# More on-chip tiles in a two-layer encoder: B's outputs kept in SBUF, spare tiles for four kinds of intermediate, a descriptor scratch of 1 KB

## The chip, the cores and the metric

The kernel runs on one core of one Trainium2 chip. The metric is the time of one execution on the device in microseconds. The core's engines are named as in the profile: PE (TensorE, with PEld for its weight loads), DVE (VectorE), ACT (ScalarE), POOL (GpSimd) and SP (SyncE, which here only issues transfers). SBUF is the on-chip memory of 128 partitions, PSUM the eight banks in which TensorE accumulates.

## The reference

A trunk of two layers over 1024 tokens of width 1024, in float32. Each layer has four groups of attention heads side by side, whose outputs (256 columns each) are joined, and an MLP of width 4096:

```python
h = rms_norm(x, norm1_g[l]); proj = h @ w_in[l]
y_a = mla_mixer(...)    # A: 4 heads, dense, keys and values from a latent of 128
y_b = diff_mixer(...)   # B: 4 heads, dense, difference of two softmaxes, rms_norm per head
y_c = swa_mixer(...)    # C: 4 query heads on 2 key heads, window of +-128 tokens, sink logits
y_d = na_mixer(...)     # D: 4 heads, 8 x 16 neighbourhood on a grid 64 wide, position bias
mix = concatenate([rms_norm(y_a), y_b, rms_norm(y_c), rms_norm(y_d)])
x = x + mix @ w_out[l]
h = rms_norm(x, norm2_g[l])
x = x + square(relu(h @ w_up[l])) @ w_down[l]
```

After the last layer there is one more rms_norm.

## The kernel before

Everything is held transposed: features on the 128 partitions, tokens along the row. A float32 product is made in three passes of a reduced format: each operand is split into a high part (a copy on ACT, L193) and a low part (a subtraction on DVE or POOL, L187), and `passes` (L219 to L221) issues high x high, high x low and low x high into one PSUM bank.

**Order of a layer.** The projections of B come first. Then four attention groups follow, B, D, C, A, and each is woven with other matrix work as filler: B with the projections for A's latent and for D, D with the projections for C and the expansion of A's latent (`latp`, `kan`, `qan`), C and A with those parts of the output projection whose inputs are there (`groups_bd`, which adds onto four tiles `sum`). Projections go through a tile `part`, are split into a tile `both` (high and low side by side) and are stored from there to DRAM as `qd`, `kd`, `vd`, `qc`, `kan`, `qar` and so on; the heads load them back as `stack` and `v`. Then come the rest of the output projection, the MLP's first half and its second half.

**A banded head (D and C).** Per block kb of 128 keys: the scores four blocks ahead (L987, bank `sb`, three banks), a softmax on DVE and ACT into `p`, up to three transposes of `p` on PE (L996, bank `tr`, two banks), the split of the result into `pth` (ACT) and `ptl` (DVE), and the product with the values (L1008 and L1009) into the one bank `pv`. After block 4 the bank is full: `pv_out` copies its upper half to a tile `pvt` (ACT, L757), DVE adds both halves into the output tile `y` (in C `yc`, from another pool), PE zeroes the bank again (L1037), and the blocks 3 and 4, which were held, are applied to the second half. `pvt` shares its tiles with `ptl`.

**B's outputs.** When a pair of B's heads is finished, `sub_norm` normalises its tile `y`, stores it to DRAM as `yb` (SP, L166) and lets the tile go; `mix_b` loads it back into a tile `rz` (L159) during D and splits it, scaled, into `mixh` and `mixl` (ACT L196, DVE L197) for the output projection. B has two such tiles, D two, A two; the pool holds two tiles `y` in all.

**The MLP's first half.** The product with `w_up` is made by a scheme of seven products for two by two blocks. For each of 16 column groups q seven block products (p1 to p7, "12", "11" and so on) are accumulated in banks and moved to result tiles `ev` of 128 x 512 (ACT L1237 for the second product, L1247 and L1256 for two others), which are activated (DVE L1220, ACT L1222), combined by four subtractions (L187, `ev<-ev`) and stored to DRAM as `acts`, by ACT's queue or SP's (L1226). The groups 0 and 1 run together, product by product; from group 2 on they run one by one, with the last three products of the group before in between.

**What sets the order.** In the attention a scheduler orders each engine's instructions by a modelled timeline and by the priorities that the weave gives. In the MLP the order on PE is the order in which the code is written; the other engines are scheduled. A tile is taken from a pool of `bufs` tiles of its tag; the first write into a tile waits until the work on its former content is done, loads and stores included.

Of the kernel before, what the change touches and what calls it, by code (L numbers as in the profile page):

```python
# [13 lines left out]
F = mybir.dt.float32  # L14
R = mybir.dt.float32r
# [4 lines left out]
P = 128  # L20
S = 1024
# [123 lines left out]
class Trunk:  # L145
# [436 lines left out]

    def both(self):

        return self.pp.tile([P, 2, 512], R, tag="both", bufs=2, name="both")

    def emit_parts(self, src, dst, rows=slice(0, P), scale=None):

# [114 lines left out]
    def latent_up(self, l, lat, rows, qa, ka, va):  # L703
# [30 lines left out]

        w0 = self.weights(d["w_lat"][l, 0])
        yield from two([w0[0], both(w0[1])], parts[0:2], self.ev_rope(tabs, qr))
        plain = lambda r, dst: self.ev_plain(r, self.to_parts(dst))
        yield from two([w0[2], both(w0[3])], parts[0:2], plain(rq, qn[:, 0]))
        w1 = self.weights(d["w_lat"][l, 1])
        yield from two(w1[2:3], parts[2:3], plain(rkv, kn[:, 0]))  # L740
        w2 = self.weights(d["w_lat"][l, 2])
        for t in range(2):
            yield from two(w2[t:t + 1], parts[2:3], self.ev_plain(rkv, self.to_values(va[2 * t:2 * t + 2])))
        yield from two([w1[0], both(w1[1])], parts[0:2], plain(rq, qn[:, 1]))
        yield from two(w1[3:4], parts[2:3], plain(rkv, kn[:, 1]))

# [6 lines left out]

    def pv_out(self, pv, y, j, half, grid=False):

        t = self.ap.tile([P, 512], R, tag="ptl", bufs=3, name="pvt").bitcast(F)[0:64]
        self.nc.scalar.activation(t, pv[64:128], AF.Copy)  # L757
        a, b, o = pv[0:64], t, y[j * 64:(j + 1) * 64]
        if grid:
            a, b = (v.rearrange("p (b r c) -> p b r c", b=4, r=16) for v in (a, b))  # L760
            o = o.rearrange("p (r b c) -> p b r c", b=8, c=8)[:, 4 * half:4 * half + 4]
        else:
            o = o[:, half * 512:half * 512 + 512]
        self.tt(o, a, b, ALU.add)
# [25 lines left out]
        return self.ap.tile([P, S], F, tag="rz", bufs=2, name="rz")  # L790

    def ypair(self):
        return self.ap.tile([P, S], F, tag="y", bufs=2, name="y")

    def ptile(self):
        return self.ap.tile([P, S], F, tag="p", bufs=self.NP, name="p")
# [5 lines left out]

    def transposed(self, w):

        return [self.ap.tile([P, 512], R, tag=n, bufs=3, name=n)[:, :w] for n in ("pth", "ptl")]


    def softmax(self, passes, qt, z, scale):
# [106 lines left out]
    def sub_norm(self, y, rz, out):  # L915

        nc = self.nc
        self.tt(y, y, rz, eng=nc.gpsimd)
        yield
        sq = self.rz_tile()  # L920
        nc.scalar.activation(sq, y, AF.Square)
        r = self.rstd_cols(sq, 64, self.pairs, eng=nc.gpsimd)
        yield
        r = self.rows_of(r)
        yield
        rb = self.rz_tile()
        for h2 in range(2):
            self.spread(rb[h2 * 64:(h2 + 1) * 64], r, h2, 2)
        yield
        self.tt(y, y, rb, eng=nc.gpsimd)  # L930
        kept = self.dram.tile([P, S], F, tag="yb", bufs=2, name="yb")
        self.keep(kept, y)
        out.append(kept)
        yield

    def attn_a(self, l, qa, kn, krd, va, ys):
# [177 lines left out]

    def mix_b(self, mix, ys, g):
        for t, y in enumerate(ys):
            yt = self.rz_tile()
            self.load(yt, y)
            yield
            mix[t] = self.mixed(yt, g)  # L1120
            yield

    def mix_group(self, mix, k0, ys, g, eng=None):
# [34 lines left out]
    def piece(self, tag, dt=F, name=None):  # L1158


        pool = self.late if tag in ("c", "ev") else self.early
        return pool.tile([P, 512], dt, tag=tag, bufs={"raw": 10, "ev": 9}.get(tag, 8), name=name or tag)

    def rows_split(self, t, src, scale=None):

# [335 lines left out]
```

## Time and profile before

| | before |
|---|---|
| time, median of 3 runs | 2698.26 us (2697.42 to 2702.37) |
| the profiled execution's time | 2701.14 us |
| its span, first to last instruction | 2698.9 us |
| mean granted clock of TensorE | 0.969 |
| TensorE busy | 2545.4 us, 94% |
| VectorE, ScalarE, GpSimd busy | 1944.6, 1438.1, 1151.6 us |
| moved by DMA | 389.18 MB |

A row of the timeline gives start, duration, engine, line, operation, output <- inputs, size, and in brackets the idle time just before it and what ended it. A row of the waits gives who waited for what: total, times, longest, in us. A row of the table by stage gives the stage's bounds and length, each engine's busy time with its count of instructions, the granted clock as a share of full speed, the mean busy share of the DMA engines, and GB/s. In layer 0, D and C run from about 330 to 505 us and the MLP from 700; in layer 1, D and C from about 1660 to 1835 and the MLP from 2030.

### The profile page before, as it was taken

The numbers are of one execution on the slowest core, as the hardware profiler recorded it, in microseconds if no ns is written. First come the engines' busy times: TensorE is split into PE (matmuls) and PEld (weight loads), VectorE is DVE, ScalarE is ACT, GpSimd is POOL, SyncE is SP. The second block draws the span as 40 slices with busy tenths as digits, with TensorE's granted clock in tenths as the row PEclk, the third lists the DMA queues.
The fourth block names the chain that finished last, engine by engine and source line by source line (L and its number), as shares of the span: only waits on it lengthen the run. The fifth ranks groups of instructions, "written<-read, shape, count | busy, mean of one in ns | idle before, by whom it ended". The sixth has DMA issues, their size and how long they took to land.

```text
span 2698.9 us, 37585 instructions
## 1 busy us (share of the span) xinstructions
PE 2545.4 (94%) x12296; PEld 2109.5 (78%) x12296; DVE 1944.6 (72%) x3368; ACT 1438.1 (53%) x2591; POOL 1151.6 (43%) x816
## 2 busy tenths in 40 slices
PE   8999988999889999999999999789998999999997
PEld 6778876787778887888877788677886788778886
DVE  6777767784966669887568776577749666687776
ACT  4677756663534444444437776566635344444444
POOL 2555633301345554544425655332013455545552
PEclk9989998999999999999999899899999999999998
DMA  5534597421144457444245436963221444664431
GB/s 171 174 94 141 151 268 245 106 89 57 53 140 153 150 166 269 149 139 142 100 128 149 119 114 192 273 199 89 71 71 55 156 150 151 230 219 150 131 102 63
DMA packets 191666, 389.18 MB, mean 144 GB/s; under 512 B 23840, under 2 KB 33008, under 8 KB 191472
## 3 DMA queue, kind: packets, MB, share of 16 engines
q1 hardware_dynamic: 177648, 361.62, 43.3%
q10 hardware_dynamic: 13824, 25.17, 2.7%
q8 instruction: 97, 1.59, 0.2%
q14 instruction: 97, 0.79, 0.1%
HBM read 263.29 MB, written 123.41 MB: 143 GB/s over the span
## 4 chain that ended last, share of the span: by engine, by line
PE 73%; DVE 13%; DMA 5%; ACT 5%; issue 3%; POOL 1%; SPq 0%; DVEq 0%; ACTq 0%; POOLq 0%
PE u L219 8%; PE u L221 8%; PE u L220 8%; PE mm L219 6%; PE mm L220 5%; PE mm L221 5%; PE p L219 5%; PE p L220 5%; PE p L221 5%; PE sb L815 3%; DVE p L817 2%; DVE part L187 2%; PE tr L851 2%; ACT p L820 2%; DVE ptl L187 1%
## 5 line engine op out<-in xcount | busy, mean ns | idle before, releaser
L187 POOL TENSOR_TENSOR wl<-raw,wh 128x512 fp32r<-128x512 f32 x448 | 636.0, 1420 | 699.0 <-ACT wh L193 680.1
L193 ACT ACTIVATE wh<-raw 128x512 fp32r<-128x512 f32 x448 | 281.6, 629 | 575.0 <-PE u L220 314.6
L187 POOL TENSOR_TENSOR wl<-ws,wh 128x512 fp32r<-128x512 f32 (+1 forms) x120 | 151.2, 1262 | 431.2 <-ACT wh L193 427.1
L219 PE MATMUL u<-far,wh 128*128 128x512 f32 x768 | 301.5, 393 | 12.6 <-ACT ev L1247 8.3
L187 DVE TENSOR_TENSOR ptl<-tr,pth 128x512 fp32r<-128x512 f32 (+2 forms) x384 | 239.2, 629 | 88.4 <-ACT pth L193 87.2
L221 PE MATMUL u<-far,wl 128*128 128x512 f32 x768 | 300.8, 392 | 0.8 <-POOL wl L187 0.8
L187 DVE TENSOR_TENSOR raw<-raw 128x512 f32<-128x512 f32 x256 | 222.7, 875 | 107.9 <-POOL wl L187 54.2
L220 PE MATMUL u<-far,wh 128*128 128x512 f32 x768 | 300.5, 391 | 0.0
L193 ACT ACTIVATE pth<-tr 128x512 fp32r<-128x512 f32 (+2 forms) x384 | 206.2, 547 | 123.1 <-PE tr L851 67.2
L820 ACT ACTIVATE p<-p,nm 128x1024 f32<-128x1024 f32 x192 | 220.2, 1147 | 77.3 <-DVE nm L817 72.8
L219 PE MATMUL p<-far,wh 128*128 128x512 f32 x640 | 252.3, 394 | 7.5 <-DVE ev L187 7.5
L221 PE MATMUL p<-far,wl 128*128 128x512 f32 x640 | 251.0, 392 | 1.5 <-POOL wl L187 1.5
L220 PE MATMUL p<-far,wh 128*128 128x512 f32 x640 | 251.2, 392 | 0.0
L815 PE MATMUL sb<-stack 96*128 96x512 f32 x640 | 217.6, 422 | 13.1 <-DVE nm L817 12.8
L187 DVE TENSOR_TENSOR far<-act,far 128x512 fp32r<-128x512 f32 x224 | 210.4, 969 | 14.6 <-ACT far L193 14.6
L187 POOL TENSOR_TENSOR p<-p 128x1024 f32<-128x1024 f32 x64 | 153.5, 2402 | 110.8 <-ACT p L903 103.0
L219 PEld LDWEIGHTS u<-far,wh 128*128 128x128 f32 x768 | 145.4, 189 | 45.2 <-ACT ev L1247 9.2
L851 PE MATMUL tr<-ident,p 128*128 128x128 f32 x1024 | 163.2, 278 | 8.8 <-DVE ptl L187 6.0
L221 PEld LDWEIGHTS u<-far,wl 128*128 128x128 f32 x768 | 145.1, 189 | 32.2 <-POOL wl L187 1.6
L219 PE MATMUL mm<-xh,wh 128*128 128x512 f32 x416 | 168.3, 405 | 1.4 <-DVE part L187 1.2
L220 PEld LDWEIGHTS u<-far,wh 128*128 128x128 f32 x768 | 145.3, 189 | 30.1
L220 PE MATMUL mm<-xl,wh 128*128 128x512 f32 x416 | 165.3, 397 | 0.0
(248 smaller groups left out, 6110.1 us busy)
## 6 DMA issues: line engine op xcount, KB each, us to landing
act<-acts SPq DMA_DIRECT2D x224, 256.0 KB
raw<-in_w_up SPq DMA_DIRECT2D x128, 256.0 KB
acts<-ev SPq DMA_DIRECT2D x128, 256.0 KB
raw<-in_w_down SPq DMA_DIRECT2D x128, 256.0 KB
acts<-ev ACTq DMA_DIRECT2D x96, 256.0 KB
ws<-in_w_in SPq DMA_DIRECT2D x76, 256.0 KB
rz<-drows SPq DMA_DIRECT2D x40, 256.0 KB
stack<-kd SPq DMA_DIRECT2D x32, 256.0 KB
```

The source lines that it names most:

```text
L187: (eng or self.nc.vector).tensor_tensor(out=out, in0=a, in1=b, op=op)
L193: nc.scalar.activation(hi, src, AF.Copy)
L219: mm(ps, w[0], x[0][:, sl], start=start, stop=False)
L220: mm(ps, w[0], x[1][:, sl], start=False, stop=False)
L221: mm(ps, w[1], x[0][:, sl], start=False, stop=stop)
L815: self.nc.tensor.matmul(ps, q[:, qt * P:(qt + 1) * P], k[:, sl], start=i == 0, stop=i == len(passes) - 1)
L817: self.nc.vector.tensor_tensor_reduce(out=p[:, sl], in0=ps, in1=self.zero[:, 0:1].bitcast(F).broadcast_to([P, 512]), scale=-scale, scalar= ...
L820: self.nc.scalar.activation(p, p, AF.Exp, bias=nm[:, 1:2], scale=-1.0, accum_out=z)
L851: nc.tensor.transpose(t[:, k * 256 + i * P:k * 256 + (i + 1) * P], p[:, (j * 2 + k) * P:(j * 2 + k + 1) * P], self.ident)
```

## The change

Five things, in one diff:

- B's output tiles are no longer stored and loaded again: `sub_norm` hands on the tile itself, `mix_b` reads it (and so gives way once less per tile), and the pool holds four tiles `y` instead of two.
- `both` has three tiles instead of two.
- `pth`, `ptl` and with it `pvt` have four tiles each instead of three.
- The MLP has 13 result tiles `ev` instead of nine.
- The program is made with a dynamic DMA scratch of 1024 bytes.

Per partition that is 8 KB more for `y`, 4 KB for `both`, 4 KB for `pth` and `ptl` together, and 8 KB more for `ev` in the MLP.

```diff
     def both(self):
-        return self.pp.tile([P, 2, 512], R, tag="both", bufs=2, name="both")
+        return self.pp.tile([P, 2, 512], R, tag="both", bufs=3, name="both")
...
     def pv_out(self, pv, y, j, half, grid=False):
-        t = self.ap.tile([P, 512], R, tag="ptl", bufs=3, name="pvt").bitcast(F)[0:64]
+        t = self.ap.tile([P, 512], R, tag="ptl", bufs=4, name="pvt").bitcast(F)[0:64]
...
     def ypair(self):
-        return self.ap.tile([P, S], F, tag="y", bufs=2, name="y")
+        return self.ap.tile([P, S], F, tag="y", bufs=4, name="y")
...
     def transposed(self, w):
-        return [self.ap.tile([P, 512], R, tag=n, bufs=3, name=n)[:, :w] for n in ("pth", "ptl")]
+        return [self.ap.tile([P, 512], R, tag=n, bufs=4, name=n)[:, :w] for n in ("pth", "ptl")]
...
         self.tt(y, y, rb, eng=nc.gpsimd)
-        kept = self.dram.tile([P, S], F, tag="yb", bufs=2, name="yb")
-        self.keep(kept, y)
-        out.append(kept)
+        out.append(y)
         yield
...
     def mix_b(self, mix, ys, g):
         for t, y in enumerate(ys):
-            yt = self.rz_tile()
-            self.load(yt, y)
-            yield
-            mix[t] = self.mixed(yt, g)
+            mix[t] = self.mixed(y, g)
             yield
...
-        return pool.tile([P, 512], dt, tag=tag, bufs={"raw": 10, "ev": 9}.get(tag, 8), name=name or tag)
+        return pool.tile([P, 512], dt, tag=tag, bufs={"raw": 10, "ev": 13}.get(tag, 8), name=name or tag)
...
-    nc = bacc.Bacc("TRN2", target_bir_lowering=False, num_devices=1)
+    nc = bacc.Bacc("TRN2", target_bir_lowering=False, num_devices=1, dynamic_dma_scratch_size=1024)
```

Line numbers fall by 2 to 5 behind the deleted lines (L996 becomes L994, L1008 L1006, L1037 L1035, L1237 L1232). The number of instructions on PE, DVE, ACT and POOL is the same; SP issues eight transfers fewer. The scheduler orders the attention anew on every engine; in the MLP the order on PE is the same.

On PE, in the third head of D of layer 0, around the change from the first half of `pv` to the second (L1037, then L1035), before:

```order
L987 MATMUL sb<-stack 128x384 x4
L1008 MATMUL pv<-pth,v 128x128
L1009 MATMUL pv<-ptl,v 128x128
L996 MATMUL tr<-ident,p 128x128 x3
L1037 MATMUL pv<-zero 128x512
L1008 MATMUL pv<-pth,v 128x128
L1009 MATMUL pv<-ptl,v 128x128
L1008 MATMUL pv<-pth,v 128x256
L1009 MATMUL pv<-ptl,v 128x256
```

and with the change:

```order
L1007 MATMUL pv<-ptl,v 128x128
L994 MATMUL tr<-ident,p 128x128 x3
L647 MATMUL mm<-ident,part 128x128 x4
L275 MATMUL mm<-ident,rz 8x128
L994 MATMUL tr<-ident,p 128x128 x2
L219 MATMUL mm<-latp,wh 128x512
L220 MATMUL mm<-latp,wh 128x512
L221 MATMUL mm<-latp,wl 128x512
L731 MATMUL mm<-latp,wh 128x512 x2
L1035 MATMUL pv<-zero 128x512
L1006 MATMUL pv<-pth,v 128x128
L1007 MATMUL pv<-ptl,v 128x128
```

Between the last product of the first half and the zeroing there now stand the transposes of one more block and filler (four transposes of values, a projection of `latp`) beside the three transposes that stood there.

On ACT, in D of layer 1, where the first of B's outputs is mixed (L196), before:

```order
L757 ACTIVATE pvt<-pv 64x512
L193 ACTIVATE both<-part 128x512
L193 ACTIVATE pth<-tr 128x384 x2
L196 ACTIVATE mixh<-rz,g_sub 128x512 x2
L1066 ACTIVATE p,z_17118<-p,nb 128x384 x2
L193 ACTIVATE pth<-tr 128x384 x2
```

and with the change:

```order
L1064 ACTIVATE p,z_16473<-p,nb 128x384
L722 ACTIVATE wh<-wl 64x128
L1064 ACTIVATE p,z_16473<-p,nb 128x384
L193 ACTIVATE pth<-tr 128x384
L196 ACTIVATE mixh<-y,g_sub 128x512 x2
L193 ACTIVATE wh<-ws 128x512
L193 ACTIVATE pth<-tr 128x384 x2
```

The mixing reads `y` instead of `rz`, and it now stands one head of D earlier; copies `pth<-tr` follow it in both.

On SP, in group C of layer 0, from the load of the values of C's second key head (`v<-vc`) to the loads of the four partial sums, before:

```order
L159 DMA v<-vc 128x1024
L166 DMA kan<-both 128x2x512
L159 DMA rz<-drows 64x1024
L162 DMA drows<-rows 8x16x8
L166 DMA kan<-both 128x2x512
L159 DMA stack<-kan 64x1024
L162 DMA drows<-rows 8x16x8
L159 DMA stack<-krd 32x1024
L159 DMA stack<-qan 64x1024
L159 DMA rz<-drows 64x1024
L159 DMA stack<-qar 32x1024
L159 DMA sum<-in_x 128x1024 x4
```

and with the change:

```order
L166 DMA kan<-both 128x2x512
L159 DMA rz<-drows 64x1024
L159 DMA ws<-in_w_out 128x256
L159 DMA rz<-drows 64x1024
L159 DMA sum<-in_x 128x1024 x4
L159 DMA v<-vc 128x1024
L159 DMA stack<-kan 64x1024
```

The load of the values now stands behind the four loads of the sums, and the same is so in layer 1.

## The prediction

> **What bounds the kernel now.** I read the page first: busy time, then the chain that ended last.
>
> ```profile
> PE 2545.4 (94%) x12296; PEld 2109.5 (78%) x12296; DVE 1944.6 (72%) x3368; ACT 1438.1 (53%) x2591; POOL 1151.6 (43%) x816
> PE 73%; DVE 13%; DMA 5%; ACT 5%; issue 3%; POOL 1%; SPq 0%; DVEq 0%; ACTq 0%; POOLq 0%
> ```
>
> TensorE sets the time. The change gives it no matmul less, so it can only shorten what is not matmul: 2698.9 - 2545.4 = 153.5 us of idle time, and time at a reduced granted clock. The second view is busy time by stage. The first three rows are the groups D and C of layer 0, the next three the same of layer 1, then the middle of a first MLP half, and three pieces of ten microseconds.
>
> ```profile
> core 0: us, PE busy (x) PEld busy (x) DVE busy (x) ACT busy (x) POOL busy (x), PEclk, DMA share, GB/s
> 330.00:380.00 50.00, 45.81 (x244) 38.97 (x242) 25.35 (x62) 24.68 (x62) 21.27 (x14) 0.93 0.90 253
> 380.00:440.00 60.00, 49.68 (x279) 42.18 (x280) 47.63 (x121) 42.47 (x112) 21.91 (x20) 0.91 0.92 281
> 440.00:505.00 65.00, 57.62 (x298) 47.88 (x297) 46.40 (x117) 39.42 (x99) 19.57 (x18) 0.89 0.56 159
> 1660.00:1712.00 52.00, 45.40 (x243) 38.89 (x241) 26.17 (x67) 26.60 (x64) 20.94 (x13) 0.93 0.93 262
> 1712.00:1775.00 63.00, 53.94 (x286) 46.27 (x287) 47.07 (x123) 41.64 (x110) 19.54 (x20) 0.86 0.86 260
> 1775.00:1835.00 60.00, 50.77 (x267) 41.85 (x267) 42.99 (x104) 37.07 (x92) 18.51 (x18) 0.91 0.57 170
> 770.00:1015.00 245.00, 245.00 (x1077) 201.97 (x1076) 156.27 (x187) 102.33 (x180) 129.08 (x90) 1.00 0.46 153
> 410.00:420.00 10.00, 6.08 (x23) 4.51 (x23) 4.48 (x12) 3.99 (x11) 1.36 (x1) 0.66 1.04 308
> 420.00:430.00 10.00, 9.08 (x52) 7.30 (x53) 10.00 (x26) 8.93 (x24) 2.13 (x1) 1.00 0.88 309
> 1740.00:1750.00 10.00, 5.50 (x22) 4.55 (x21) 5.75 (x13) 5.64 (x15) 0.00 (x0) 0.66 1.03 332
> ```
>
> D and C leave TensorE idle for 175 - 153.1 = 21.9 us in layer 0 and 175 - 150.1 = 24.9 us in layer 1, at a clock of 0.86 to 0.93, with the DMA engines 90% busy. The MLP's middle (770 to 1015) has no gap at all: more MLP results can do nothing there. So the places to look at are D and C, where all the spare tiles but one kind are added, and the edges of the MLP. The third view says what TensorE waits for there, layer 0 first:
>
> ```profile
> PE pv L1008 <- ACT pth L193: 5.6, 5, 2.4
> PE pv L1037 <- DVE y L187: 4.6, 2, 3.0
> PE mm L220 <- DMA latp<-lat: 3.2, 1, 3.2
> PE pv L1037 <- DVE yc L187: 3.0, 1, 3.0
> PE pv L1009 <- DVE ptl L187: 1.9, 2, 1.6
> ```
>
> and layer 1:
>
> ```profile
> PE pv L1008 <- ACT pth L193: 4.9, 4, 2.4
> PE mm L220 <- DMA latp<-lat: 4.7, 1, 4.7
> PE pv L1037 <- DVE y L187: 2.3, 4, 1.4
> ```
>
> **The change part by part.** The sum is made against the profiled execution (2701.14 us, 2.9 above the median of 2698.26; its span is 2698.9) and the gain is then taken off the median.
>
> *MLP results, 9 tiles to 13.* Where the first two column groups end and the third begins, TensorE stops:
>
> ```profile
> 764.54 0.80 PE L219 MATMUL u<-oph,wh 128*128 128x512 f32 x1 [3.84 <-ACT ev L1237]
> 2092.00 7.18 DVE L187 TENSOR_TENSOR ev<-ev 128x512 f32<-128x512 f32 x8
> 2097.33 0.60 ACT L1237 ACTIVATE ev<-u 128x512 f32<-128x512 f32 x1 [2.69 <-DVE ev L187]
> 2097.98 0.71 PE L219 MATMUL u<-oph,wh 128*128 128x512 f32 x1 [3.84 <-ACT ev L1237]
> ```
>
> The copy of the third group needs a free result tile. In the program of before it waits for the fifth of these subtractions, which ends just ahead of it; in the changed program for the third. Five of the eight take 2097.33 - 2092.00 = 5.33 us, 1.07 each, so the copy and the matmul behind it come 2.1 us earlier, in both layers: **4.2 us**. The other copies that TensorE waits for in the MLP wait for matmuls, not tiles, and stay. Bounds: 0, if another subtraction ends last, and 2 x 3.84 = 7.7.
>
> *B's outputs stay on chip.* The change removes four stores and four loads of 512 KB, 4 MB in all:
>
> ```profile
> L166 SPq DMA_DIRECT2D yb<-y x4: 319/334/344, 307.2 to 1739.6; - x4
> L159 SPq DMA_DIRECT2D rz<-yb x4: 325/425/700, 399.6 to 1749.0; - x4
> 413.70 0.68 DVE L187 TENSOR_TENSOR y<-pv,pvt 64x512 f32<-64x512 f32 x1 [2.68 <-DMA yb<-y]
> 414.44 0.80 PE L1037 MATMUL pv<-zero 128*128 128x512 f32 x1 [3.00 <-DVE y L187]
> 1739.58 1.34 ACT L196 ACTIVATE mixh<-rz,g_sub 128x512 fp32r<-128x512 f32 x2 [1.20 <-DMA rz<-yb]
> 1742.54 0.39 PE L1008 MATMUL pv<-pth,v 128*128 128x256 f32 x1 [2.37 <-ACT pth L193]
> ```
>
> In layer 0 D's second output tile is one of B's, and VectorE could not write it until the store of B's had landed: TensorE lost 3.00 us. Four tiles for y take that reason away. What stays is the plain wait of the zeroing for the evacuation ahead of it, here (4.6 + 2.3 - 3.0) / 5 = 0.8 us each: 2.2 us gained. In layer 1 ScalarE waits 1.20 us for the reload and works 1.34 us on it while the copy of D's probabilities, for which TensorE waits 2.37 us, stands behind. With y on chip that mixing has its data already, and in the changed program it stands behind a different head's work; of 2.37 us I take 1.9 (bounds 0, when the 1.34 us still stands ahead of such a copy, and 2.37). Both stalls lie in the windows with a clock of 0.66. There (1 - 0.66) x 6.08 = 2.1 and (1 - 0.66) x 5.50 = 1.9 us of busy time come from the slower clock. Sum: 2.2 + 1.9 + 2.1 + 1.9 = **8.1 us** (bounds 0 and 9.4).
>
> [...]
>
> *Stored parts, 2 tiles to 3.* Two splits wait for an earlier store out of the same tile:
>
> ```profile
> 397.06 0.63 ACT L193 ACTIVATE both<-part 128x512 fp32r<-128x512 f32 x1 [2.74 <-DMA qar<-both]
> 398.25 0.69 PE L1008 MATMUL pv<-pth,v 128*128 128x384 f32 x1 [1.65 <-ACT pth L193]
> 1746.52 0.60 ACT L651 ACTIVATE both<-mm 128x512 fp32r<-128x512 f32 x1 [0.53 <-DMA kan<-both]
> 1747.90 0.79 PE L219 MATMUL mm<-latp,wh 128*128 128x512 f32 x1 [2.13 <-DVE both L187]
> ```
>
> In the first, the transposed parts' copy is queued on ScalarE behind the waiting split, and TensorE behind that: 1.65 us. In the second ScalarE waited only 0.53 us. **2.2 us** (bounds 0 and 1.65 + 2.13 = 3.8).
>
> *Transposed parts and pvt, 3 tiles to 4.* The waits for pth, y, yc and ptl above add up to 5.6 + 4.6 + 3.0 + 1.9 + 4.9 + 2.3 = 22.3 us; less the 1.65, 3.00 and 2.37 already used, 15.3 remain. They are chains of dependence: a transpose, its copy on ScalarE, the product; or the single bank pv, its evacuation, the next zeroing. A fourth tile shortens none of them; it lets the scheduler put other work in front, as it does at one of D's half changes, where the transposes of the next block now stand ahead of the zeroing, but not at all. Bounds 0 (or a loss of one 3.00 us stall, if the order puts a chain in the open that is covered now) and 15.3. Nearer to the low end, since the rows are latencies: 30%, **4.6 us**.
>
> *Less traffic.* One queue carries all of it (D's part of layer 0):
>
> ```profile
> q1 hardware_dynamic: 12852, 29.42, 91.0%
> ```
>
> At 29.42 MB in 110 us, or 267 GB/s, 4 MB are 15.7 us of transfer, nearly all under matmuls. The direct waits for data, latp's 3.2 + 4.7 us, begin before most of that traffic. **1 us** (bounds 0 and 7.9).
>
> *The scratch of 1 KB* is room only: the transfers shown are issued by SP and ACT. It costs 0; what it buys is the tiles above.
>
> *Sum and what is late next.* The four attention terms make 8.1 + 2.2 + 4.6 + 1.0 = 15.9 us. They can't all be kept. VectorE is 10.00 of 10.00 us busy from 420 to 430, right behind the removed stall of layer 0, and where a stall goes, the next chain (transpose, ScalarE, VectorE, bank pv) is the one that ends last. I keep two thirds, 10.6 us, and 4.2 of the MLP: 14.8 us. 2701.14 - 14.8 = 2686.3 profiled, and 2698.26 - 14.8 = 2683.5: **2683 us**.
>
> **Rivals.** (1) *Hidden anyway.* The removed waits in D and C are replaced by the next ones of the same chains, since ScalarE and VectorE are 70 to 80% busy there, and the new order is no better than the old. Only the MLP's 4.2 us stay, or less if the third subtraction isn't the last thing waited for: 2694 to 2698. For it: 15.3 of 22.3 us are latencies. Against it: three of the stalls have a transfer as their cause, and the transfer goes or its tile is no longer shared. That the tiles lie unused belongs here.
>
> (2) *Everything opens.* The spare tiles decouple D and C so far that all terms reach their bounds: 7.7 + 9.4 + 3.8 + 15.3 + 7.9 = 44 us, 2654; with 80% of that, 2663. For it: 46.8 us of idle time in D and C beside a lowered clock. Against: the banks in PSUM stay as they are, three for scores, two for transposes, one for products.
>
> (3) *Slower: a load of group C stands behind four others.* In the changed order SP issues the values of C's second key head behind the four loads of partial sums, 2 MB; now it is ahead of them.
>
> ```profile
> 439.23 0.33 SPq L159 DMA_DIRECT2D v<-vc  x1
> 448.20 1.84 SPq L159 DMA_DIRECT2D sum<-in_x  x4
> 468.98 0.31 PE L1008 MATMUL pv<-pth,v 128*128 128x128 f32 x1
> ```
>
> The third row is the first product that needs it. Five tiles of 512 KB at the 159 GB/s of this stage (440 to 505) take 16.5 us; issued at 450 they land by 466.5, 2.5 us ahead of the need. It decides only if the loads are 2.5 us later against the products than now. SP issues in order, so a wait of SP ahead of them does that. If they come 10 us late in each layer, with 2 us for the clock after, the loss is 24 us against the gain of 14.8: +9.2, about 2707. Against it: in that stage the DMA engines are only 56% busy.
>
> **How the numbers follow.** A measurement of this kernel can't tell less than 0.2% (5.4 us) from no change. The forecast's case, a gain of 5.4 to 27 us, has 0.60; rival (1) 0.16; rival (2) 0.15; rival (3) 0.09. The forecast and (2) are faster, 0.75; (1) is the same, 0.16; (3) slower, 0.09. The forecast's own range is 2671 to 2693; reaching to most of (1) and part of (2) until 0.2 is left out, it is 2666 to 2697.
>
> **What would show it.** The matmul of 764.54 and 2097.98 should wait some 1.7 us instead of 3.84, and 3.84 again would show the MLP term wrong. No row may name yb, no ScalarE split in D should wait for a store out of the stored parts, and the ten microseconds around the former 414.44 and 1742.54 should have a clock above 0.9. The idle time of D and C should fall from 21.9 and 24.9 to about 17 and 20. Wrong it would be if that idle time is as before with other names in the wait lists (rival 1), if it falls under 12 a layer (rival 2), or if a product of group C waits for v (rival 3).

## The result and the profile after

Five runs of each on the same chip gave 2702.37 us before (2697.42 to 2707.92) and 2684.88 us with the change (2680.53 to 2691.32): a ratio of 0.9938, 95% interval 0.9918 to 0.9958, or 17.5 us less. The forecast was 2683.

The profiled execution of the change took 2691.32 us and was the slowest of its five; its span is 2689.5 us, 9.4 less than the one profiled before. Its trace shows which waits went, less well how much. From the page, busy time:

```profile
PE 2538.6 (94%) x12296; PEld 2098.8 (78%) x12296; DVE 1939.3 (72%) x3368; ACT 1436.1 (53%) x2591; POOL 1146.9 (43%) x816
```

The same number of matmuls took 2545.4 - 2538.6 = 6.8 us less, and the idle time fell from 153.5 to 150.9, only 2.6. The granted clock, 0.969 before, is 0.975 now. The busy time by stage of the change, in the six stretches of D and C that the prediction shows and then the two places that had a clock of 0.66 (a transfer counts whole where it starts, so the DMA share of a short stretch can pass 1):

```profile
core 0: us, PE busy (x) PEld busy (x) DVE busy (x) ACT busy (x) POOL busy (x), PEclk, DMA share, GB/s
330.00:380.00 50.00, 44.92 (x251) 38.82 (x250) 30.35 (x68) 25.77 (x63) 22.79 (x15) 0.97 0.87 254
380.00:440.00 60.00, 50.94 (x278) 41.29 (x278) 44.40 (x117) 42.35 (x111) 23.09 (x23) 0.94 0.99 296
440.00:505.00 65.00, 57.90 (x313) 47.45 (x313) 49.94 (x125) 41.44 (x101) 14.75 (x15) 0.95 0.41 118
1660.00:1712.00 52.00, 46.89 (x266) 40.80 (x266) 31.51 (x71) 29.27 (x70) 24.39 (x16) 0.95 0.99 276
1712.00:1775.00 63.00, 52.62 (x283) 42.36 (x281) 46.17 (x125) 44.32 (x118) 23.26 (x22) 0.93 0.95 301
1775.00:1835.00 60.00, 53.62 (x281) 45.22 (x281) 42.80 (x107) 36.84 (x90) 11.85 (x14) 0.91 0.34 90
410.00:420.00 10.00, 7.37 (x45) 6.14 (x44) 6.93 (x16) 5.22 (x12) 1.25 (x2) 1.00 1.04 294
1740.00:1750.00 10.00, 8.83 (x52) 7.41 (x53) 8.47 (x20) 7.09 (x19) 0.74 (x2) 1.00 1.04 325
```

In five of the six stretches of D and C the clock rose, from 0.93, 0.91, 0.89, 0.93 and 0.86 to 0.97, 0.94, 0.95, 0.95 and 0.93; in the sixth it is 0.91 in both. The two tens of microseconds with 0.66 have 1.00, with 45 and 52 matmuls in them instead of 23 and 22. No row names yb. The MLP's edge, in the timeline of the change:

```profile
755.64 0.60 ACT L1232 ACTIVATE ev<-u 128x512 f32<-128x512 f32 x1 [0.42 <-DVE ev L187]
756.29 0.50 PE L219 MATMUL u<-oph,wh 128*128 128x512 f32 x1 [1.57 <-ACT ev L1232]
2088.74 0.51 PE L219 MATMUL u<-oph,wh 128*128 128x512 f32 x1 [1.80 <-ACT ev L1232]
```

The waits of 3.84 us are 1.57 and 1.80 now. In D and C other waits stand where the old ones were. Rows of TensorE's waits from D's first score to A's, first layer 0:

```profile
PE tr L994 <- DVE ptl L187: 5.7, 5, 3.3
PE mm L220 <- DMA latp<-lat: 3.3, 1, 3.3
PE pv L1035 <- DVE y L187: 1.3, 3, 0.7
```

then layer 1:

```profile
PE pv L1006 <- ACT pth L193: 5.0, 4, 2.8
PE pv L1007 <- DVE ptl L187: 3.8, 2, 3.2
PE mm L219 <- DVE rows L277: 2.7, 1, 2.7
```

The zeroing waits 1.3 us instead of 4.6 in layer 0. New are two waits for VectorE's `ptl` of over 3 us, one in each layer. The timeline of the change shows what is in front of it:

```profile
455.64 4.68 POOL L187 TENSOR_TENSOR y<-y,rz 128x1024 f32<-128x1024 f32 x2 [6.28 <-DMA rz<-drows]
458.06 1.33 ACT L196 ACTIVATE mixh<-y,par 128x512 fp32r<-128x512 f32 x2 [2.64 <-POOL y L187]
458.81 2.06 DVE L197 SCALAR_TENSOR_TENSOR mixl<-y,par,mixh 128x512 fp32r<-128x512 f32 x1 [1.53 <-ACT mixh L196]
460.80 0.41 DVE L187 TENSOR_TENSOR ptl<-tr,pth 128x256 fp32r<-128x256 f32 x1
461.36 0.45 PE L994 MATMUL tr<-ident,p 128*128 128x128 f32 x1 [3.32 <-DVE ptl L187]
...
1770.64 1.29 DVE L187 TENSOR_TENSOR sum<-mm,sum 128x512 f32<-128x512 f32 x2 [2.44 <-DMA sum<-saved]
1771.84 0.55 DVE L187 TENSOR_TENSOR ptl<-tr,pth 128x384 fp32r<-128x384 f32 x1
1772.45 0.69 PE L1007 MATMUL pv<-ptl,v 128*128 128x384 f32 x1 [3.25 <-DVE ptl L187]
```

At 461 the mixing of D's outputs, late because a reload from DRAM was late, stands on VectorE ahead of `ptl`. At 1770 VectorE stands still for the load of a partial sum with `ptl` behind it. The kernel before has the same wait for a partial sum, 2.45 us at 1791.35, and TensorE stood 2.24 us behind that one too; what is new is that `ptl` stands there. These rows read as a matter of which instruction the scheduler put in front of which. So the first thing to find out was what part of the gain is due to the tiles, and what part to the order.

### The profile page after: what moved, and what is told of

It reads as the page before. It is cut to its first block, busy times and chain, and to the rows that moved or that the text cites. A ratio compares the mean times of both kernels' runs of the same rounds, so it can differ in the third digit from the quotient of the medians.

```text
span 2689.5 us, 37453 instructions
## 1 busy us (share of the span) xinstructions
PE 2538.6 (94%) x12296; PEld 2098.8 (78%) x12296; DVE 1939.3 (72%) x3368; ACT 1436.1 (53%) x2591; POOL 1146.9 (43%) x816
## 5 line engine op out<-in xcount | busy, mean ns | idle before, releaser
L187 DVE TENSOR_TENSOR far<-act,far 128x512 fp32r<-128x512 f32 x224 | 208.6, 960 | 14.6 <-ACT far L193 14.6
L187 POOL TENSOR_TENSOR p<-p 128x1024 f32<-128x1024 f32 x64 | 153.5, 2403 | 126.9 <-ACT p L903 107.6
L851 PE MATMUL tr<-ident,p 128*128 128x128 f32 x1024 | 163.0, 278 | 10.5 <-DVE ptl L187 6.3
L817 DVE CUSTOM_DVE_ANT_0 p<-sb,zero 128x512 f32<-128x512 f32 x192 | 128.7, 685 | 58.8 <-PE tr L851 21.7
```

The lines of the kernel that those rows point to most:

```text
L187: (eng or self.nc.vector).tensor_tensor(out=out, in0=a, in1=b, op=op)
L817: self.nc.vector.tensor_tensor_reduce(out=p[:, sl], in0=ps, in1=self.zero[:, 0:1].bitcast(F).broadcast_to([P, 512]), scale=-scale, scalar= ...
L851: nc.tensor.transpose(t[:, k * 256 + i * P:k * 256 + (i + 1) * P], p[:, (j * 2 + k) * P:(j * 2 + k + 1) * P], self.ident)
```

## The experiments

All were timed in five rounds against the kernel before, on one chip within each set. All with a part alone have the small scratch too; the scratch alone was not run. (The first of them has, in layer 0's attention, the order of the kernel before on every engine.) Times are medians, ratios come with 95% intervals.

**Each part alone.** First the MLP's tiles:

```diff
-bufs={"raw": 10, "ev": 9}
+bufs={"raw": 10, "ev": 13}
```

> The kernel before with 13 result tiles in the MLP (and the small scratch that makes room) and nothing else. The prediction's term: the wait of 3.84 us at the third column group falls to about 1.7 in both layers, -4.2 us in all. If the attention alone makes the gain, the time stays within 1 us of before. If the gain of the whole is a matter of the new order of the attention, this one, which leaves that order nearly as it is, still shows -4.2 and no more.

Measured: 2692.96 us against 2701.12, ratio 0.9973 (0.9958 to 0.9988), 7 us faster, between 3 and 11. The term is real, and the 4.2 us of the forecast lie in that range.

B's outputs on chip:

```diff
-tag="y", bufs=2
+tag="y", bufs=4
...
-        kept = self.dram.tile([P, S], F, tag="yb", bufs=2, name="yb")
-        self.keep(kept, y)
-        out.append(kept)
+        out.append(y)
...
-            yt = self.rz_tile()
-            self.load(yt, y)
-            yield
-            mix[t] = self.mixed(yt, g)
+            mix[t] = self.mixed(y, g)
```

> The kernel before with B's outputs kept on chip and four tiles y, nothing else. The prediction's term: the waits for the store and for the reload of yb go, -8 us before any haircut, some -5 with it; the clock of the stretches around the former waits is above 0.9. If those waits are hidden anyway, 0 to -2 with other names in the wait lists of D and C. If the order decides, anything between -10 and +5, with the difference spread over stretches where yb was never waited for.

Measured: 2697.70 us, ratio 0.9994 (0.9979 to 1.0010): no difference that can be told. The waits for yb were gone. The clock of the ten microseconds from 410 and from 1740, expected above 0.9, was 0.83 in both. The timeline of this kernel shows a wait that the kernel before does not have:

```profile
399.92 0.42 DVE L1061 CUSTOM_DVE_ANT_0 p<-sb,bias 128x256 f32<-128x256 f32 x1 [3.73 <-DMA bias<-in_bias]
400.41 0.65 PE L985 MATMUL sb<-stack 128*128 128x384 f32 x1 [3.19 <-DVE nb L1061]
```

The fourth head of D waits for its position bias, of which there is one tile, loaded anew for each head. That is a transfer which the change doesn't touch. In the kernel before the same instruction of VectorE starts at 398.89, with no wait ahead of it. The new wait stands 14 us ahead of the place where the wait for yb was, so it is not that wait's successor; that it came with the new order is likely, and not shown.

The stored parts:

```diff
-tag="both", bufs=2
+tag="both", bufs=3
```

> The kernel before with three tiles for the stored parts, nothing else. The prediction's term: -2.2 us (at most -3.8), in D. If the order decides, a change of several us of either sign, in stretches without a wait for a store out of the stored parts.

Measured: 2707.92 us, ratio 1.0024 (1.0011 to 1.0038): 6.5 us **slower**. In D and C of layer 0 ScalarE's waits for a store out of these tiles, 5.2 us in the kernel before, are gone; in layer 1 they are 4.0 us instead of 3.1. So the term's waits went in one layer, and the loss lies elsewhere.

The transposed parts and pvt:

```diff
-tag="ptl", bufs=3, name="pvt"
+tag="ptl", bufs=4, name="pvt"
...
-tag=n, bufs=3, name=n
+tag=n, bufs=4, name=n
```

> The kernel before with four tiles each for the transposed parts and pvt, nothing else. The prediction's term: -4.6 us out of 15.3 us of waits in D and C, since these waits are latencies of a chain and only the order around them can move. If the chains are latencies through and through, 0. If the order decides, several us of either sign, in the groups B and A as well, which use the same tiles.

Measured: 2705.76 us, ratio 1.0011 (0.9997 to 1.0025): not faster. The four parts alone add up to -0.27 - 0.06 + 0.24 + 0.11 = +0.02%; together they give -0.62%. They don't add up.

**The change without one part each.** The edits are the four above, taken back one at a time.

> The change without the MLP's part (nine result tiles again). By the prediction and by the run with that part alone: 4 to 7 us slower than the change, some 9 to 13 us faster than before, and the waits of 3.84 us back.

Measured: 2685.70 us against 2704.33, ratio 0.9933 (0.9914 to 0.9951), and not 4 to 7 us slower than the change. The waits of 3.84 us are back, and in the profiles the MLP takes 8 us longer than in the change, while D, C and A are 10 us shorter. Of these 10 us 4 lie in layer 0, where the order is that of the change on every engine, and the change's profile is of its slowest execution. So a new order can't be given the whole, and what makes up for the 8 us stays open.

> The change with B's outputs stored and loaded again (two tiles y). If the parts only work together because B's outputs free the transfers and the tile y for the others, this gives the whole attention gain back: about 2693, only the MLP's part left. If they add up, it is 2 us slower than the change.

Measured: 2690.98 us, ratio 0.9948 (0.9928 to 0.9969). Most of the gain stays, with all eight transfers of yb back. Yet nothing waits for yb in D and C of this kernel, and the clock from 330 to 435 and from 1660 to 1765 is 0.95 and 0.97 here, after 0.92 and 0.89 before: with the other spare tiles and their order these waits go without the change that was to remove them.

> The change with two tiles for the stored parts again. If the parts add up as measured alone, this is 6 us faster than the change, since alone the third tile cost 6.5 us. If what was measured alone is the draw of an order, it comes out anywhere within some 8 us of the change.

Measured: 2681.42 us, ratio 0.9919 (0.9901 to 0.9937).

> The change with three tiles for transposed parts and pvt again. If the parts add up, 3 us faster than the change. If the fourth tile pays once the other waits are gone, 5 us or more slower. If the order decides, within some 8 us of either side.

Measured: 2686.09 us, ratio 0.9935 (0.9916 to 0.9955). No part can be named whose absence takes the gain away: any two of the three attention parts keep it, while each of them alone, in the one order that it was run in, shows none.

**The order alone.** The weave gives group B's main work a priority lead of 40. At 42 or 38 all work and all tiles are the same and the scheduler orders the attention anew:

```diff
-    NP, RB, RD, LB, LD = 6, (7, 8), (3, 2), 40, 50
+    NP, RB, RD, LB, LD = 6, (7, 8), (3, 2), 42, 50
```

and with 38 likewise. This was done to the kernel before and to the changed one.

> The kernel before with the priority lead of group B's main work at 42 instead of 40: the same tiles and the same work, but the scheduler orders the attention anew. If a new order alone is a draw that moves the time by some 7 us either way, this one lies within 2694 to 2708 and not at 2701; if the gain of the change comes from the order alone, one of the two reordered kernels of before may come near 2686. If the gain comes from the tiles, both stay above 2694.

Measured: 2712.92 us against 2699.80, ratio 1.0048 (1.0036 to 1.0060).

> The kernel before with that lead at 38: a second order with the same tiles. As for the first: above 2694 if the tiles make the gain, near 2686 if an order can make it alone.

Measured: 2707.57 us, ratio 1.0023 (1.0013 to 1.0033).

> The changed kernel with that lead at 42: its tiles, another order. If the tiles make the gain, within 7 us of the change and clearly faster than before, by 10 to 24 us. If the change's order was a lucky draw, it falls back to the MLP's part, 5 us faster than before (2696).

Measured: 2682.17 us, ratio 0.9932 (0.9919 to 0.9945).

> The changed kernel with that lead at 38: a second order with its tiles. As for the first: 10 to 24 us faster than before if the tiles make the gain, about 2696 if its order did.

Measured: 2686.24 us, ratio 0.9945 (0.9933 to 0.9957).

With the old tiles a new order costs 8 to 13 us; with the new tiles it moves the time by a few. At equal lead the change is worth 2712.92 - 2682.17 = 31 us (42), 21 us (38) and 17.5 us (40). So the tiles make the gain, not a lucky order. Of its three orders the kernel before stood on the best; that part of what the tiles give pays for leaving it fits this, but three orders don't show it.

**By stage.** From the profiles of all fourteen kernels, cut at the first score product of a group and the first and last products into `u` of an MLP. "B" is everything from the start of a layer to D's first score, "D, C, A" from there to the MLP; both layers are added, in brackets TensorE's idle time:

| kernel | B | D, C, A | MLP |
|---|---|---|---|
| before | 657.2 (32.4) | 761.5 (65.4) | 1280.1 (55.6) |
| before, lead 42 | 663.9 (37.8) | 765.5 (75.8) | 1283.6 (58.4) |
| before, lead 38 | 661.9 (33.8) | 760.8 (67.2) | 1283.6 (57.3) |
| MLP results alone | 665.3 (37.8) | 759.4 (65.2) | 1274.6 (53.4) |
| B's outputs alone | 655.1 (34.5) | 759.3 (61.4) | 1280.5 (55.2) |
| stored parts alone | 661.2 (33.6) | 766.4 (66.2) | 1280.6 (56.3) |
| transposed parts alone | 658.3 (32.5) | 763.2 (64.2) | 1286.1 (59.4) |
| the change | 665.0 (39.2) | 749.7 (59.0) | 1274.8 (52.7) |
| without MLP results | 661.5 (38.0) | 739.8 (52.3) | 1282.8 (57.3) |
| without B's outputs | 658.7 (34.5) | 744.0 (56.7) | 1275.5 (53.2) |
| without stored parts | 658.0 (33.6) | 751.7 (59.7) | 1273.9 (51.6) |
| without transposed parts | 663.2 (39.8) | 749.1 (55.2) | 1273.6 (53.6) |
| the change, lead 42 | 665.4 (35.0) | 739.8 (50.6) | 1272.5 (52.7) |
| the change, lead 38 | 664.8 (35.0) | 744.9 (58.5) | 1274.6 (52.5) |

Each row is one execution, up to 11 us off the median of its kernel (without B's outputs: 2680.03 against 2690.98). The kernel before and the one with the MLP's results alone have the same order in D, C and A on every engine; yet the second is 3 us longer there in layer 0 and 5 us shorter in layer 1. So rows a few microseconds apart can't be told from each other, and the means below carry the argument.

The column of D, C and A splits the kernels without overlap: 759.3 to 766.4 us with none or one of the three attention parts (mean 762.3), 739.8 to 751.7 with two or three (mean 745.6), 16.7 us less. 66.5 - 56.0 = 10.5 us of that is idle time, the other 6 shorter busy time of the same matmuls, that is, a higher clock (0.961 and 0.975 over this stage). The MLP column splits as cleanly by its tiles: mean 1282.5 with nine, 1274.2 with 13, 8.3 us less, of which 57.1 - 52.8 = 4.3 us is idle time. Column B is no better, and 2 us longer on the mean, which is no more than the scatter of its rows.

What more tiles do in D can be seen in one stretch of 105 us in each layer, at the same times in every kernel; it begins 2 to 13 us behind D's first score. Busy time by stage, before:

```profile
330.00:435.00 105.00, 90.49 (x494) 76.94 (x493) 68.82 (x170) 62.52 (x161) 40.49 (x32) 0.92 0.92 269
1660.00:1765.00 105.00, 89.65 (x473) 76.95 (x472) 64.52 (x167) 60.94 (x156) 35.95 (x29) 0.89 0.92 267
```

the change:

```profile
330.00:435.00 105.00, 92.22 (x504) 77.01 (x503) 71.61 (x176) 63.57 (x164) 43.90 (x37) 0.95 0.93 277
1660.00:1765.00 105.00, 93.49 (x519) 78.38 (x518) 70.75 (x180) 67.35 (x174) 43.57 (x35) 0.95 0.97 286
```

and the change with the lead at 42:

```profile
330.00:435.00 105.00, 96.52 (x523) 81.65 (x523) 75.60 (x189) 68.84 (x176) 46.51 (x38) 0.93 0.98 287
1660.00:1765.00 105.00, 95.54 (x539) 79.29 (x538) 76.01 (x196) 72.07 (x187) 42.79 (x35) 0.98 0.97 290
```

In the same time 504 and 519, then 523 and 539 matmuls are done instead of 494 and 473. Counted over 105 us from each kernel's own first score of D, it is 506 and 506, then 530 and 545, instead of 492 and 471. DMA moves 277 to 290 GB/s instead of 267 to 269, though the kernel moves 4 MB less in all. That does not make the gain: the stored parts alone have 278 and 287 GB/s with 476 and 490 matmuls, and the change without their third tile, which has the lowest ratio, has 259 and 251 GB/s with 514 and 485.

What stays open is why one part alone brings nothing and any two bring nearly all. A stretch limited by several things in turn (the store out of the stored parts, the output tile, the transposed parts, the bias load) may show nothing until two of them are loosened. The order is a rival that was not tested here: each part alone also has a new order, a new order with the old tiles cost 0.23% and 0.48%, and a part that brought as much as that would show nothing. Against it stands the column of D, C and A, which is no shorter with one part. A part alone at other leads, which would tell, was not run.

## Why the prediction was right, and where not

**The size** was right: 14.8 us forecast, 17.5 measured, and the range held it. That it came so near is in good part luck, for of its terms only the MLP's stall came out as it was worked out.

*MLP results, 4.2 us forecast.* The mechanism is as told, and the wait fell to 1.57 and 1.80 us, where about 1.7 was named. The idle time gained is 4.3 us by the table. The stage gained 8.3, the kernel with this part alone 7 (3 to 11). The failed step is that the term stopped at the stall: in D a stall was charged with the clock behind it, in the MLP not. Busy time by stage behind the stalls of 764.54 and 2097.98, before:

```profile
764.50:768.00 3.50, 3.46 (x8) 2.79 (x9) 2.53 (x5) 0.63 (x1) 0.00 (x0) 0.50 0.93 313
764.50:775.00 10.50, 10.46 (x34) 8.38 (x35) 2.62 (x6) 2.38 (x4) 2.59 (x2) 0.72 0.50 175
2098.00:2108.50 10.50, 10.50 (x39) 8.49 (x40) 3.67 (x6) 2.92 (x6) 2.58 (x2) 0.84 0.50 177
```

and with the change, around the one of 756.29 and behind the one of 2088.74:

```profile
755.00:768.00 13.00, 10.92 (x47) 8.66 (x48) 8.00 (x10) 4.20 (x8) 5.28 (x4) 1.00 0.60 205
2088.70:2099.20 10.50, 10.46 (x39) 8.44 (x40) 5.51 (x9) 2.87 (x5) 2.97 (x3) 0.84 0.71 236
```

One of the two shorter stalls lost no clock, the other as much as before. Taken over all fourteen kernels and both layers, the 10.5 us behind this stall have a mean clock of 0.79 with nine tiles (0.71 to 0.85 in all 14 places, stalls of 3.8 to 4.8 us) and 0.93 with 13 (1.00 in eight places, 0.84 or 0.85 in six, stalls of 1.6 to 2.6 us). (0.93 - 0.79) x 10.5 = 1.5 us for each layer, 3 of the 4 us that the stage gained beside its idle time.

*B's outputs, 8.1 us before the haircut.* Both named stalls went and the clock there is 1.00, as said; the price was wrong. Alone the part is worth a few us or nothing (the time moves by -6 to +3), and the change without it keeps most of its gain. The step that failed is to price a removed stall by its own length and the clock behind it. With that part alone both stalls are gone, but the clock there is 0.83, another head waits 3.19 us for its bias, and no gain shows. The charge for the clock also put the 0.66 down to the stall of 414.44. But the clock had fallen from 1.00 to 0.50 at 411.92, half a microsecond into that stall of 3.00 us, and in the 3.41 us ahead of 411.92 TensorE was busy for 1.01. So the rows don't show that the 0.66 belongs to that stall alone.

*Stored parts, 2.2 us.* Wrong in sign for the part alone (+6.5 us, 3 to 10), although its waits went in layer 0; what it lost by stays open. Taking it out of the change gives 2681.42 against 2684.88, in the same direction, though the two intervals of the ratios overlap. In the whole change the waits did not go, as the prediction said they would; ScalarE in D of layer 0:

```profile
398.69 0.63 ACT L193 ACTIVATE both<-part 128x512 fp32r<-128x512 f32 x1 [1.75 <-DMA qan<-both]
421.40 0.63 ACT L193 ACTIVATE both<-part 128x512 fp32r<-128x512 f32 x1 [2.83 <-DMA va<-both]
```

The DMA engines are 99% busy from 380 to 440 us there; a split still finds its tile not yet stored.

*Transposed parts and pvt, 4.6 us.* Alone between 1 us faster and 7 slower. That these waits are latencies which no tile shortens fits this, and the share of 30% had no row behind it.

*Less traffic, 1 us.* The wait for `latp` stays in layer 0 (3.3 us after 3.2) and is gone in layer 1 (4.7). With B's outputs alone, where the same traffic is gone, it is 3.9 and 3.1; so less traffic does not take it away.

*The sum and the haircut.* The four terms, 15.9 us cut to 10.6, were taken as additive. They are not: each alone gives about nothing, two or three together 16.7 us in D, C and A on the mean. The total came out near because the errors met: a term that was too low (the MLP's clock), an attention gain of the whole which the terms don't explain, and a new order, which the sum has at nothing and which cost the kernel before 8 and 13 us where it alone was changed. In the profiled pair D, C and A take 11.8 us less, the MLP 5.3 less and B 7.8 more, all of it in layer 1. That the new order makes B longer is not shown: the kernel with the MLP's results alone, whose order on TensorE differs there from the one before in 49 places, takes 9 us more in the same place.

*D and C's idle time* was to be about 17 and 20 us. From D's first score to A's, by the cut of the table, it went from 19.3 and 25.4 to 19.9 and 20.7; in the prediction's own stretches it went from 21.9 and 24.9 to 21.2 and 21.9. The fall is in layer 1 alone, and layer 0 has the sign of rival (1), as much idle time under other names. With the lead at 42 it is 16.4 and 14.6 by the table's cut. What D and C gained beside it is clock, 0.86 to 0.93 in the six stretches before and 0.91 to 0.97 with the change. (The DMA engines were called 90% busy in D and C; the prediction's own rows have 0.56 and 0.57 in two of the six.)

*The rivals.* (1), that the next wait takes over, fits each part alone, as a new order does, and layer 0 of the change. (2) did not come. (3), group C's values behind the partial sums: the order is as shown, but the trace of the change names nothing that waits for these values. The wait of VectorE for a partial sum is as long as before, 2.44 and 2.45 us.

Of the versions measured, the change without the third tile for stored parts (0.9919, 0.9901 to 0.9937) and the change with the lead at 42 (0.9932, 0.9919 to 0.9945) have the best ratios. Both beat the kernel before; that either beats the change (0.9938, 0.9918 to 0.9958) can't be told.

## What to carry to other kernels

Where a scheduler sets the order, one extra tile is two changes, a wait less and another order; run the same tiles in two or three other orders, before and after, ahead of believing a difference of half a per cent. Spare tiles that show nothing one by one may gain together, as here, so test them in groups too. And price a stall of the matrix engine with the clock behind it, everywhere or nowhere: here, at the MLP's edge, the mean clock of the 10.5 us behind the stall was 0.79 with nine result tiles and 0.93 with 13.

## What the hardware showed that was not expected

Behind the same instruction of the MLP's edge in fourteen kernels, a stall of 3.8 to 4.8 us was followed by a granted clock of 0.50 to 0.55 over the next 3.5 us each time; a stall of 1.6 to 2.6 us by 0.52 to 0.69 in six places of 14 and by 1.00 in the other eight. The length alone doesn't sort these: 1.80 us lost clock and 2.57 did not. What decides was not shown. Busy time by stage in rows of 3.41 us, which is how long the clock stayed at 0.50 behind the first of these two: the stall of 1.80 us in the change (two rows) and the one of 2.57 us in the change without the third tile for stored parts (three rows):

```profile
2085.81:2089.23 3.42, 1.62 (x7) 1.03 (x7) 3.38 (x4) 1.23 (x2) 1.94 (x2) 1.00 0.66 210
2089.23:2092.64 3.41, 3.41 (x10) 2.63 (x9) 3.37 (x6) 0.00 (x0) 0.00 (x0) 0.50 0.94 321
749.77:753.18 3.41, 2.61 (x12) 1.83 (x10) 3.38 (x4) 1.25 (x3) 1.76 (x2) 1.00 0.29 77
753.18:756.59 3.41, 1.64 (x7) 1.38 (x8) 3.38 (x5) 0.88 (x2) 1.80 (x1) 1.00 0.81 241
756.59:760.01 3.42, 3.42 (x17) 2.81 (x16) 3.12 (x5) 0.23 (x1) 0.00 (x0) 1.00 1.01 337
```

The first stall lies in one row, which has 1.80 us of idle time, and the clock behind it is 0.50; the second is split over two rows, with 0.80 and 1.77, and the clock stays at 1.00. Idle time counted by such rows doesn't sort other places of the traces. In the change, layer 0, D and C:

```profile
444.00:447.42 3.42, 3.08 (x26) 2.70 (x24) 2.12 (x4) 1.69 (x7) 0.21 (x1) 1.00 1.04 289
447.42:450.83 3.41, 3.36 (x13) 2.84 (x13) 3.00 (x9) 2.59 (x8) 0.81 (x4) 0.50 0.76 187
```

and in the kernel before, at the start of the same layer's MLP:

```profile
722.53:725.95 3.42, 1.59 (x7) 0.94 (x5) 2.69 (x4) 3.12 (x6) 1.31 (x1) 1.00 0.00 0
725.95:729.36 3.41, 1.10 (x5) 0.94 (x6) 3.41 (x5) 3.41 (x8) 1.28 (x1) 1.00 0.00 0
```

A row with 0.34 us of idle time was followed by 0.50, one with 1.83 by 1.00. What was measured is the count: with this stall at 1.6 to 2.6 us instead of 3.8 to 4.8, no clock was lost behind it in eight of 14 places.
